# Keeping split weights in DRAM for the second half of the tokens

## The chip, the cores and the metric

One core of one Trainium2 chip runs the kernel. The metric is the time of one execution on the device, in microseconds; of several runs the median is given. The engines are TensorE (PE in the profile, its weight loads PEld), VectorE (DVE), ScalarE (ACT), GpSimd (POOL) and SyncE (SP). SP computes nothing here: it issues most of the DMAs, in its own order, and waits before each until what that DMA needs is there.

## The reference

It is one layer of a decoder trunk over 2048 tokens of width 1024. A normalized input is multiplied by one wide matrix, and the columns go to four recurrent mixers, whose outputs are gated, merged by a second matrix and normalized.

```python
u = rmsnorm(h, norm_w[l])
proj = (u @ w_in[l]).astype(f32)
...
y_a = gla_branch(a_q, a_k, a_v, a_gr, a_z, ...)
y_b = mlstm_branch(b_q, b_k, b_v, b_i, b_f, b_o, b_z, ...)
y_c = hgrn2_branch(c_q, c_f, c_i, c_z, lower_bounds[l], ...)
y_d = ssd_branch(d_x, d_B, d_C, d_dt, d_z, ...)
mixed = jnp.concatenate([y_a, y_b, y_c, y_d], axis=-1)
h = h + mixed @ w_out[l]
return rmsnorm(h, final_norm_w)
```

Everything is float32. The mixers run in chunks, with a state carried from one to the next.

## The kernel before, in words

**Products in three passes.** TensorE takes operands of a rounded float32 type (F32R). To keep the accuracy, each matrix is split: hi is the rounded value, lo the rounded rest (value minus hi). A product is then the sum of three matmuls, hi with hi, hi with lo and lo with hi, accumulated in PSUM. The input is split into `uh` and `ul`, the weights into `hi` and `lo`.

**Two halves.** The loop over `self.hf` in `run` takes the tokens in two halves of 1024. Each half runs ten units in the order g0, g1 (GLA), s0, s1 (SSD), h0 to h3 (HGRN2), m0, m1 (mLSTM). The projection columns stand in groups of 256, `("gqk", 0)`, `("gv", 0)` and so on, 30 for each half. Group `("gv", 0)` has 32 more columns for the gates (`wg`), so 288. The weights of a group are [128, 8, 256] float32, 1 MB, 8 KB in each partition. Both halves need the same weights. After the halves, the output stage multiplies by the second matrix.

**Loading a group.** `weights(key)` gives the split weights of a group and at once calls `load_w` for the next group of `worder`. `load_w` loads `raw` by a DMA on SP (line 224, for the gates 226), casts it to `hi` by four instructions on ACT (line 228) and subtracts to `lo` by two on POOL (line 230). There is one `raw` buffer and there are two each of `hi` and `lo`, so the split of a group waits for TensorE to have left the buffers of the group before last. The very first group comes in five pieces (lines 216 to 220), between the loads of the input tiles `xT` (line 153), which land in the small shared buffers `t2k`, of which there are five.

**The mixers.** In `lin_unit` (GLA, HGRN2) DVE multiplies `kb` and `qf` by decays (lines 496, 497), TensorE makes score tiles, and DVE and ACT put them into `ST`. In `ssd` DVE makes the decay tile at line 884, ACT the exponential at 885, DVE the product at 886, and TensorE goes on with that; each pass needs the next `ab` load (line 859). In `mlstm` line 766 copies the state. `store` (line 616) sends finished tiles from a `t2k` buffer to `y` in DRAM. `gates` holds a scan on DVE (line 363). The statistics of the rows (`row_stats`, line 169) need eight x tiles before the first projected values can be scaled.

**What sets the order.** The code's order is not the engines' order. The framework places each engine's instructions by its own estimate of when they can run, so the projection of the next group is mixed with the recurrence of the unit before it. Each engine, and SP with its DMAs, then runs its list strictly in order.

Of the kernel before, what the change touches and what calls it, by code (L numbers as in the profile page):

```python
# [10 lines left out]
F32 = mybir.dt.float32  # L11
F32R = mybir.dt.float32r
# [9 lines left out]
P = 128  # L22
S = 2048
D = 1024
KT = D // P
# [7 lines left out]
WG = 256  # L33
NG = 32
# [11 lines left out]
def _groups():  # L46
    g = {}
    cols = []

    def add(key, c):  # L50
        g[key] = len(cols)
        cols.append(c)

    for p in range(2):
        add(("gv", p), _r(GV + 256 * p, 256))
        add(("gqk", p), _r(GQ + 128 * p, 128) + _r(GK + 128 * p, 128))
        add(("gz", p), _r(GZ + 256 * p, 256))
    for h in range(4):
        add(("hqf", h), _r(HQ + 128 * h, 128) + _r(HF + 128 * h, 128))
        add(("hvz", h), _r(HV + 128 * h, 128) + _r(HZ + 128 * h, 128))  # L60
    for h in range(4):
        add(("mqk", h), _r(MQ + 128 * h, 128) + _r(MK + 128 * h, 128))
        add(("mvo", h), _r(MV + 128 * h, 128) + _r(MO + 128 * h, 128))
        if h % 2 == 0:
            add(("mz", h // 2), _r(MZ + 128 * h, 256))
    for q in range(2):
        add(("sx", q), _r(SX + 256 * q, 256))
        add(("sbc", q), _r(SB + 128 * q, 128) + _r(SC + 128 * q, 128))
        add(("sz", q), _r(SZ + 256 * q, 256))
    return g, cols  # L70


GIDX, GCOLS = _groups()
# [43 lines left out]
class Kernel:  # L117
# [79 lines left out]
    def weights(self, key):  # L197
# [4 lines left out]
            self.load_w(self.worder[nxt][1])  # L202
        return w

    def load_w(self, key, cuts=None):

        nc = self.nc
        gates = key == ("gv", 0)
        n = WG + (NG if gates else 0)
        raw = self.wp.tile([P, KT * (WG + NG)], F32, tag="raw", name="raw")[:, :KT * n].rearrange("p (k n) -> p k n", k=KT)  # L210
        hi = self.wp.tile([P, KT * (WG + NG)], F32R, tag="hi", name="hi", bufs=2)[:, :KT * n].rearrange("p (k n) -> p k n", k=KT)
        lo = self.wp.tile([P, KT * (WG + NG)], F32R, tag="lo", name="lo", bufs=2)[:, :KT * n].rearrange("p (k n) -> p k n", k=KT)
        self.wready[key] = hi, lo

        def part(k0, k1):
            nc.sync.dma_start(raw[:, k0:k1, :WG], self.a["w"][GIDX[key], :, k0:k1])
            if gates:
                nc.sync.dma_start(raw[:, k0:k1, WG:], self.a["wg"][:, k0:k1])
            nc.scalar.copy(hi[:, k0:k1], raw[:, k0:k1])
            nc.gpsimd.tensor_tensor(lo[:, k0:k1], raw[:, k0:k1], hi[:, k0:k1].bitcast(F32), op=ALU.subtract)  # L220

        if cuts:
            return [(k0, lambda k0=k0, k1=k1: part(k0, k1)) for k0, k1 in zip(cuts, cuts[1:] + [KT])]
        nc.sync.dma_start(raw[:, :, :WG], self.a["w"][GIDX[key]])
        if gates:
            nc.sync.dma_start(raw[:, :, WG:], self.a["wg"])
        for k0, k1 in ((0, 2), (2, 4), (4, 6), (6, 8)):
            nc.scalar.copy(hi[:, k0:k1], raw[:, k0:k1])  # L228
        for k0, k1 in ((0, 4), (4, 8)):
            nc.gpsimd.tensor_tensor(lo[:, k0:k1], raw[:, k0:k1], hi[:, k0:k1].bitcast(F32), op=ALU.subtract)  # L230

    def proj_chan(self, w, c, b):

        hi, lo = w
        ps = self.psp.tile([P, 512], F32, tag="proj", name="ps_c")
        cs = slice(c * P, (c + 1) * P)
        for k in range(KT):
            self.mm(ps, hi[:, k, cs], self.uh[b][:, k], start=k == 0, stop=False)
            self.mm(ps, hi[:, k, cs], self.ul[b][:, k], start=False, stop=False)
            self.mm(ps, lo[:, k, cs], self.uh[b][:, k], start=False, stop=k == KT - 1)  # L240
        return ps
# [770 lines left out]
    def run(self, units=None, y=None):  # L1012
        nc, tc, a = self.nc, self.tc, self.a
        pool = tc.tile_pool
        with pool(name="const", bufs=1) as cp, pool(name="small", bufs=2) as self.small, pool(name="dram", bufs=1, space=DRAM) as self.dram:
            self.y = self.dram.tile([S // P, 4, 32, DI // P, 4, 32], F32, tag="y", name="y") if y is None else y
            cf = cp.tile([P, 3 * P], F32, name="cf")
            self.ident, self.tri, self.cmask = (cf[:, i * P:(i + 1) * P] for i in range(3))
            self.mask = cp.tile([P, 768], U8, name="mask")
            self.par = cp.tile([P, a["par"].shape[1]], F32, name="par")  # L1020
            nc.sync.dma_start(self.par, a["par"])
            with pool(name="main", bufs=1) as self.up, pool(name="gs", bufs=1) as self.gs, pool(name="ps", bufs=1, space=PSUM) as psp:
                self.psp = _Tags(psp, {"proj": 4, "t": 4})
                self.up = _Tags(self.up, {"f": 2, "kb": 2, "qp": 2, "v": 2, "sz": 4})
                with pool(name="u", bufs=2) as self.upool, pool(name="w", bufs=1) as self.wp:
                    self.zero(cp)
                    self.whole = units is None
                    us = units or ["g0", "g1", "s0", "s1", "h0", "h1", "h2", "h3", "m0", "m1"]
                    keys = []
                    for u in us:  # L1030
                        j = int(u[1])
                        keys += {"g": [("gqk", j), ("gv", j), ("gz", j)], "h": [("hqf", j), ("hvz", j)], "s": [("sx", j), ("sbc", j), ("sz", j)],
                                 "m": [("mqk", 2 * j), ("mvo", 2 * j), ("mqk", 2 * j + 1), ("mvo", 2 * j + 1), ("mz", j)]}[u[0]]
                    self.worder = [(hf, k) for hf in range(NH) for k in keys]
                    self.wready = {}
                    self.stats = {}
                    self.xs = {}
                    first = self.load_w(keys[0], [0, 1, 2, 4, 6])
                    for self.hf in range(NH):
                        for b in range(2):  # L1040
                            if (self.hf, b) not in self.xs:
                                self.load_x(self.hf, b, first if (self.hf, b) == (0, 0) else ())
                        self.uh, self.ul = ([self.xs[self.hf, b][i] for b in range(2)] for i in range(2))
                        if self.hf == 0:
                            nc.sync.dma_start(cf, a["cf"][:, :3 * P])
                            self.prepare(cp)
                        for u in us:
                            self.steps = self.row_stats(self.hf + 1, ["f"] * NC, 1) if u == us[-1] and self.hf + 1 < NH else iter(())
                            {"g": self.gla, "h": self.hgrn, "m": self.mlstm_pair, "s": self.ssd}[u[0]](int(u[1]))
                            for _ in self.steps:  # L1050
                                pass
                if units is None:
                    with pool(name="wo", bufs=1) as wo:
                        self.out_phase(wo)
# [89 lines left out]
```

## Time and profile before

| | us |
|---|---|
| median of 3 runs | 2236.55 (2234.35 to 2238.48) |
| the profiled execution | 2236.62 |
| its span, first to last instruction | 2234.8 |
| first half of the tokens | 0 to 949 |
| second half | 949 to 1876 |
| output stage | 1876 to 2234.8 |

The profiled execution stands for the runs: it lies 0.07 us from their median. Its span is 1.8 us shorter than its time. A row of the timeline gives the start and the duration in us, the engine, the line, the operation, what it writes and from what, and in square brackets how long the engine stood idle before it and who released it. "x3" means that neighbouring rows of one kind are merged. SPq is SP's issuing of a DMA; its duration includes the waits between merged issues. The granted clock of TensorE is a share of its full 2.4 GHz; its lower level is 1.2 GHz.

### The profile page before, as it was taken

How to read it: one execution, taken by the hardware profiler on the slowest of the kernel's cores; microseconds unless marked ns; L12 is line 12 of the kernel's file. 1: busy time of each engine (PE TensorE's matmuls, PEld its weight loads, DVE VectorE, ACT ScalarE, POOL GpSimd, SP SyncE). 2: the span in 40 equal slices, each digit the busy share in tenths (PEclk: the TensorE clock that was granted, in tenths of full speed). 3: DMA queues.
4: the chain of work that ended last, by engine and by line, in shares of the span. 5: the costliest groups of instructions: out<-in, count | busy, mean ns of one | idle time of the engine just before them, and what ended most of it. 6: DMA issues, size and time to landing. Idle time of an engine off the chain costs nothing.

```text
span 2234.8 us, 35049 instructions
## 1 busy us (share of the span) xinstructions
PE 2113.7 (95%) x13758; PEld 1888.7 (85%) x13758; DVE 1395.2 (62%) x3325; ACT 821.5 (37%) x1763; POOL 382.7 (17%) x283
## 2 busy tenths in 40 slices
PE   8899999989999999998989899999999999999998
PEld 7888788878889998997978788888899998788887
DVE  3674878767667676636677876776676566532332
ACT  6633332344434334454323223443343334321211
POOL 3212122320111111121211222211111210000000
PEclk9999999999999999999999989999999999999999
DMA  7111212221111132420202222211121215432321
GB/s 235 56 34 44 58 47 66 69 48 48 49 49 39 49 84 106 126 75 22 58 24 62 69 46 76 54 36 43 45 76 49 56 48 175 160 111 78 113 71 48
DMA packets 186149, 156.66 MB, mean 70 GB/s; under 512 B 141944, under 2 KB 154344, under 8 KB 178688
## 3 DMA queue, kind: packets, MB, share of 16 engines
q1 hardware_dynamic: 179504, 135.02, 21.2%
q10 hardware_dynamic: 6480, 19.40, 2.4%
q8 instruction: 108, 1.77, 0.3%
q14 instruction: 57, 0.47, 0.1%
HBM read 129.11 MB, written 25.27 MB: 69 GB/s over the span
## 4 chain that ended last, share of the span: by engine, by line
PE 75%; DVE 16%; ACT 4%; DMA 2%; issue 2%; POOL 0%; SPq 0%; ACTq 0%; DVEq 0%
PE ps_t L123 26%; PE ps_c L123 19%; PE ps_out L123 15%; PE ps_o L123 6%; PE ps_s L123 4%; PE ps_u L123 2%; PE ps_g L123 2%; DVE t2k L884 2%; DVE kb L496 2%; DVE qf L497 1%; DVE xc L717 1%; DMA ST<-w_out 1%; DMA t2k<-xT 1%; DVE st L766 1%; DMA ab<-rows 1%
## 5 line engine op out<-in xcount | busy, mean ns | idle before, releaser
L123 PE MATMUL ps_t<-hi,uh 128*128 128x256 f32 x1920 | 546.5, 285 | 0.0
L123 PE MATMUL ps_t<-hi,ul 128*128 128x256 f32 x1920 | 546.0, 284 | 0.0
L123 PE MATMUL ps_t<-lo,uh 128*128 128x256 f32 x1920 | 545.1, 284 | 0.0
L230 POOL TENSOR_TENSOR lo<-raw,hi 128x1024 fp32r<-128x1024 f32 (+1 forms) x118 | 294.4, 2515 | 950.2 <-ACT hi L228 917.3
L123 PEld LDWEIGHTS ps_t<-lo,uh 128*128 128x128 f32 x1920 | 369.8, 193 | 0.9
L123 PEld LDWEIGHTS ps_t<-hi,uh 128*128 128x128 f32 x1920 | 369.6, 193 | 1.0
L123 PEld LDWEIGHTS ps_t<-hi,ul 128*128 128x128 f32 x1920 | 369.5, 192 | 1.0 <-issue 0.9
L123 PE MATMUL ps_c<-uh,hi 128*128 128x512 f32 x896 | 357.9, 400 | 7.4 <-ACT uh L155 7.4
L123 PE MATMUL ps_c<-uh,lo 128*128 128x512 f32 x896 | 358.6, 400 | 0.0
L123 PE MATMUL ps_c<-ul,hi 128*128 128x512 f32 x896 | 357.7, 399 | 0.0
L123 PEld LDWEIGHTS ps_c<-uh,hi 128*128 128x128 f32 x896 | 171.5, 191 | 40.4 <-ACT uh L155 7.8
L123 PEld LDWEIGHTS ps_c<-ul,hi 128*128 128x128 f32 x896 | 171.6, 191 | 34.7 <-DVE ul L156 0.5
L123 PEld LDWEIGHTS ps_c<-uh,lo 128*128 128x128 f32 x896 | 171.1, 191 | 33.5
L228 ACT CAST hi<-raw 128x512 fp32r<-128x512 f32 (+1 forms) x236 | 134.6, 626 | 59.6 <-issue 33.2
L956 DVE TENSOR_TENSOR o_sz<-o_sz,ps_out 128x512 f32<-128x512 f32 (+1 forms) x33 | 22.1, 671 | 130.5 <-PE ps_out L123 127.9
L123 PE MATMUL ps_out<-woh,o_qp 128*128 128x512 f32 x288 | 94.0, 394 | 0.0
L281 ACT ACTIVATE v<-ps_t,ss 128x128 f32<-128x128 f32 x128 | 39.7, 361 | 129.3 <-PE ps_t L123 129.0
L276 ACT ACTIVATE sz<-ps_t,ss 128x128 f32<-128x128 f32 (+1 forms) x160 | 53.2, 387 | 65.2 <-PE ps_t L123 58.1
L123 PE MATMUL ps_out<-woh,o_v 128*128 128x512 f32 (+1 forms) x213 | 75.4, 389 | 0.0
L277 DVE SCALAR_TENSOR_TENSOR sz<-sz,ps_t 128x256 f32<-128x256 f32 (+1 forms) x80 | 37.5, 469 | 60.7 <-ACT sz L276 60.4
L497 DVE TENSOR_TENSOR qf<-qf,pl 128x512 f32<-128x512 f32 x72 | 61.0, 847 | 21.6 <-ACT t2k L472 12.1
L496 DVE TENSOR_TENSOR kb<-kb,pl 128x512 f32<-128x512 f32 x72 | 67.9, 942 | 10.3 <-PE ps_s L123 9.4
(367 smaller groups left out, 3793.1 us busy)
## 6 DMA issues: line engine op xcount, KB each, us to landing
raw<-w SPq DMA_DIRECT2D x59, 1024.0 KB, 4.8
y<-t2k SPq DMA_DIRECT2D x256, 64.0 KB, 2.0
t2k<-y SPq DMA_DIRECT2D x64, 256.0 KB, 3.5
t2k<-xT SPq DMA_DIRECT2D x32, 256.0 KB, 3.6
ab<-rows SPq DMA_DIRECT2D x16, 512.0 KB, 5.0
o_sz<-x ACTq DMA_DIRECT2D x16, 512.0 KB, 4.5
o_f<-x SPq DMA_DIRECT2D x12, 512.0 KB, 5.3
mb<-rows SPq DMA_DIRECT2D x8, 512.0 KB, 3.6
```

What stands on the lines that cost most here:

```text
L123: self.nc.tensor.matmul(out, l, r, start=start, stop=stop, skip_group_check=shared)
L228: nc.scalar.copy(hi[:, k0:k1], raw[:, k0:k1])
L230: nc.gpsimd.tensor_tensor(lo[:, k0:k1], raw[:, k0:k1], hi[:, k0:k1].bitcast(F32), op=ALU.subtract)
L276: nc.scalar.activation(out[:, j], ps[:, j], AF.Tanh, scale=self.rsh[:, t + j:t + j + 1])
L277: nc.vector.scalar_tensor_tensor(out=out, in0=out, scalar=1.0, in1=ps, op0=ALU.add, op1=ALU.mult)
L281: self.nc.scalar.activation(out[:, j], ps[:, j], AF.Identity, scale=sc[:, t + j:t + j + 1])
L496: nc.vector.tensor_tensor(kv[:, :, 0], kv[:, :, 0], pv[:, :, 1:2].to_broadcast([P, n, b]), op=ALU.mult)
L497: nc.vector.tensor_tensor(qv[:, :, 1], qv[:, :, 1], pv[:, :, 0:1].to_broadcast([P, n, b]), op=ALU.mult)
L717: nc.vector.scalar_tensor_tensor(out=acc, in0=raw[:, k:k + TH], scalar=cw[k], in1=acc, op0=ALU.mult, op1=ALU.add)
L766: nc.vector.tensor_copy(st[:, 0, :N], car)
L884: nc.vector.scalar_tensor_tensor(out=L[:, h], in0=ab[:, h, j * C:(j + 1) * C], scalar=self.acs[:, cc, 4 * q + h:4 * q + h + 1], in1=self.c ...
L956: nc.vector.tensor_tensor(xt[:, ns], xt[:, ns], ps, op=ALU.add)
```

## The change

In the first half each group is split as before, and then `hi` and `lo` are written to scratch tensors in DRAM (`wk`, one pair per group), by two DMAs on SP. In the second half the same group finds its pair in `self.wkept`, and two DMAs on SP load `hi` and `lo` directly; there is no raw load, no cast on ACT and no subtraction on POOL. The pieces of the very first group are stored piece by piece.

```diff
+    def ahead_of(self, key):
+
+        return int(key in self.wkept)
...
         n = WG + (NG if gates else 0)
-        raw = self.wp.tile([P, KT * (WG + NG)], F32, tag="raw", name="raw")[:, :KT * n].rearrange("p (k n) -> p k n", k=KT)
...
         self.wready[key] = hi, lo
+        if self.ahead_of(key) > 0:
+            for t, d in zip((hi, lo), self.wkept[key]):
+                nc.sync.dma_start(t.bitcast(F32), d.bitcast(F32))
+            return
+        raw = self.wp.tile([P, KT * (WG + NG)], F32, tag="raw", name="raw")[:, :KT * n].rearrange("p (k n) -> p k n", k=KT)
+        self.wkept[key] = [self.dram.tile([P, KT, n], F32R, tag=f"wk{GIDX[key]}{i}", name="wk") for i in range(2)]
...
             nc.gpsimd.tensor_tensor(lo[:, k0:k1], raw[:, k0:k1], hi[:, k0:k1].bitcast(F32), op=ALU.subtract)
+            keep(k0, k1, 0)
+            keep(k0, k1, 1)
+
+        def keep(k0, k1, i):
+            nc.sync.dma_start(self.wkept[key][i][:, k0:k1].bitcast(F32), (hi, lo)[i][:, k0:k1].bitcast(F32))
...
             nc.scalar.copy(hi[:, k0:k1], raw[:, k0:k1])
+        keep(0, 8, 0)
         for k0, k1 in ((0, 4), (4, 8)):
             nc.gpsimd.tensor_tensor(lo[:, k0:k1], raw[:, k0:k1], hi[:, k0:k1].bitcast(F32), op=ALU.subtract)
+        keep(0, 8, 1)
...
+                    self.wkept = {}
```

The instructions move on each engine accordingly. In the changed kernel a line number is some 16 higher (line 616 becomes 632, 230 becomes 245, 695 becomes 711). At the start of the program SP's list before held, from the third piece of the first group on, raw pieces and input tiles alone:

```order
L216 DMA raw<-w 128x512
L153 DMA t2k<-xT 128x512 x2
L216 DMA raw<-w 128x512
L153 DMA t2k<-xT 128x512 x2
L216 DMA raw<-w 128x512
L153 DMA t2k<-xT 128x512 x5
```

The same place of SP's list now, from the fourth piece on (three stores of hi stand just ahead of these rows):

```order
L225 DMA raw<-w 128x512
L153 DMA t2k<-xT 128x512 x2
L225 DMA raw<-w 128x512
L234 DMA wk<-hi 128x512
L234 DMA wk<-lo 128x256 x2
L234 DMA wk<-lo 128x512 x2
L234 DMA wk<-hi 128x512
L234 DMA wk<-lo 128x512
L153 DMA t2k<-xT 128x512 x5
```

The seventh input tile, the first of the last row, now follows the stores of all pieces. Further on, of the eight x tiles of the row statistics three stand ahead of the stores of the gate group and five behind them.

At the change from the first half to the second, SP's list before loaded the raw weights of the gate group first, then input tiles (xT) and finished outputs (y):

```order
L224 DMA raw<-w 128x8x256
L226 DMA raw<-wg 128x8x32
L153 DMA t2k<-xT 128x512 x8
L616 DMA y<-t2k 32x16x32 x8
L153 DMA t2k<-xT 128x512 x5
L224 DMA raw<-w 128x2048
L153 DMA t2k<-xT 128x512 x3
L616 DMA y<-t2k 32x16x32 x8
```

There SP now has (2304 elements is the gate group, 2048 another group):

```order
L219 DMA hi<-wk 128x2048
L153 DMA t2k<-xT 128x512 x8
L632 DMA y<-t2k 32x16x32 x8
L153 DMA t2k<-xT 128x512 x5
L219 DMA hi<-wk 128x2304
L153 DMA t2k<-xT 128x512 x3
L632 DMA y<-t2k 32x16x32 x8
L219 DMA lo<-wk 128x2304
```

Lo of the gate group has moved behind the last eight stores, and TensorE's list has two products of that group 18 products ahead of the end of the group before it. In the second half, POOL's list before held subtractions among its other work (here from GLA to SSD):

```order
L471 MEMSET t2k 64x4x64 x6
L230 TENSOR_TENSOR lo<-raw,hi 128x1024 x2
L471 MEMSET t2k 64x4x64 x2
L230 TENSOR_TENSOR lo<-raw,hi 128x1024 x2
L695 MEMSET ST_93 128x4x128
L695 MEMSET ST_95 128x4x128
L230 TENSOR_TENSOR lo<-raw,hi 128x1024 x4
L896 TENSOR_TENSOR t2k<-t2k 128x256
L897 TENSOR_TENSOR sz<-t2k,sz 128x256
```

The same stretch of POOL's list now:

```order
L487 MEMSET t2k 64x4x64 x26
L711 MEMSET ST_93 128x4x128
L711 MEMSET ST_95 128x4x128
L912 TENSOR_TENSOR t2k<-t2k 128x256
L913 TENSOR_TENSOR sz<-t2k,sz 128x256
```

All subtractions are gone from there; the other work of POOL stands in the same order.

## Rows read from the trace of the kernel before

**Rows 1.** Busy time by stage: stretch, length, engines' busy us, granted clock, DMA share, GB/s.
```profile
0.00:949.00 949.00, 888.64 (x6133) 807.20 (x6134) 637.69 (x1505) 385.28 (x834) 204.75 (x155) 0.98 0.24 71
949.00:1876.00 927.00, 874.35 (x6069) 796.06 (x6068) 625.29 (x1461) 356.41 (x779) 177.94 (x128) 0.98 0.20 55
```
**Rows 2.** Whom TensorE waited for, 949 to 1876: us in total, times, longest us.
```profile
PE ps_o L123 <- DVE t2k L886: 13.3, 7, 3.8
PE ps_s L123 <- DVE kb L496: 7.5, 3, 3.4
PE ps_s L123 <- ACT t2k L439: 5.7, 4, 1.9
PE ps_m L386 <- DVE o_sz L363: 5.6, 1, 5.6
PE ps_u L123 <- ACT t2k L569: 4.4, 2, 4.0
...
PE ps_u L123 <- DVE rs_y L135: 4.2, 3, 1.5
```
**Rows 3.** POOL's costliest group, 949 to 1876: busy us, mean ns, idle before, releasers.
```profile
L230 POOL TENSOR_TENSOR lo<-raw,hi 128x1024 fp32r<-128x1024 f32 x56 | 139.2, 2506 | 464.5 <-ACT hi L228 461.4 <-issue 1.5 <-DVE qf L497 1.2
```
**Rows 4.** Timeline in SSD of the second half, a split beside line 884.
```profile
1226.56 4.75 POOL L230 TENSOR_TENSOR lo<-raw,hi 128x1024 fp32r<-128x1024 f32 x2 [19.26 <-ACT hi L228]
...
1226.96 4.76 DVE L884 SCALAR_TENSOR_TENSOR t2k<-ab,g_cs,cf 128x128 f32<-128x128 f32 x3
...
1233.16 1.47 PE L123 MATMUL ps_o<-t2k 128*128 128x64 f32 x8 [3.77 <-DVE t2k L886]
...
1238.98 0.60 DVE L884 SCALAR_TENSOR_TENSOR t2k<-ab,g_cs,cf 128x128 f32<-128x128 f32 x2
```
**Rows 5.** Timeline in mLSTM of the second half, POOL and DVE.
```profile
1654.19 4.74 POOL L230 TENSOR_TENSOR lo<-raw,hi 128x1024 fp32r<-128x1024 f32 x2 [19.46 <-ACT hi L228]
...
1657.11 1.91 DVE L766 COPY st<-mst 128x129 f32<-128x129 f32 x1 [0.40 <-PE ps_o L123]
...
1666.11 0.23 DVE L766 COPY st<-mst 128x129 f32<-128x129 f32 x1
```
**Rows 6.** Timeline in HGRN2 of the second half, DVE; POOL splits from 1466.57 on.
```profile
1467.60 1.91 DVE L496 TENSOR_TENSOR kb<-kb,pl 128x512 f32<-128x512 f32 x1
...
1474.04 0.70 DVE L496 TENSOR_TENSOR kb<-kb,pl 128x512 f32<-128x512 f32 x1
```
**Rows 7.** The page, DMA issues: count, KB of one, median us to landing.
```profile
raw<-w SPq DMA_DIRECT2D x59, 1024.0 KB, 4.8
...
t2k<-xT SPq DMA_DIRECT2D x32, 256.0 KB, 3.6
...
out_dram<-o_sz SPq DMA_DIRECT2D x16, 256.0 KB, 3.3
```
**Rows 8.** The chain of work that ended last: start us, us, what.
```profile
32.53 2.64 POOL lo L230
35.21 27.31 PE ps_g L123 x191
...
962.83 25.21 PE ps_g L123 x189
...
1683.34 23.03 PE ps_t L123 x192
```
**Rows 9.** Timeline of the start: SP, POOL and DVE.
```profile
8.84 6.48 SPq L153 DMA_DIRECT2D t2k<-xT  x5
...
14.41 1.70 POOL L220 TENSOR_TENSOR lo<-raw,hi 128x512 fp32r<-128x512 f32 x1 [0.66 <-ACT hi L219]
...
36.57 0.42 SPq L169 DMA_DIRECT2D o_pl<-x  x1
...
45.07 0.17 DVE L176 TENSOR_SCALAR ss<-ss 128x8 f32<-128x8 f32 x1 [14.09 <-ACT o_pl L173]
```
**Rows 10.** Timeline of the stage change: SP's last eight y stores.
```profile
955.29 5.28 SPq L616 DMA_DIRECT2D y<-t2k  x8
```

## The prediction

> **What bounds the kernel now.** The first view to read is the busy time by stage [rows 1]: TensorE is busy for 874.35 of the 927 us of the second half of the tokens and for 888.64 of 949 in the first; the output stage behind them the change doesn't touch. So the kernel is bound by TensorE, and an edit can win only what TensorE stands idle, 52.65 us in the second half, and what its clock costs. The granted clock there is 0.98 on average; between 2.4 GHz and 1.2 GHz this means some 4% of 927 us, 37 us, at the lower level, and about 18 us lost by it.
>
> The second view is who TensorE waits for in the second half [rows 2]: VectorE (DVE) and ScalarE (ACT), never GpSimd (POOL). One could conclude that the work which the change removes, 139.2 us of POOL in this stretch [rows 3] and the casts on ACT, costs nothing. The timelines say otherwise. At 1226.56 POOL begins the two subtractions of a split, and in the same 4.75 us DVE gets only three score instructions of line 884 done, 4.76 us in all; the same instruction takes 0.60 us for two when POOL is quiet, at 1238.98. TensorE, which needs that score tile, then idles 3.77 us [rows 4]. In the mLSTM part the copy of line 766 takes 1.91 us beside a split and 0.23 without [rows 5]; in HGRN2 the product of line 496 takes 1.91 us while a split runs and 0.70 a moment later [rows 6]. POOL is thus on the path through DVE, and each split is charged to TensorE in places.
>
> The Trainium skill has this as a rule ("SBUF — State Buffer", section "Who interferes with whom"): a VectorE instruction with two SBUF inputs, or in a two-port mode, and a GpSimd instruction that reads SBUF take a shared port pair as an exclusive lock, so the later one stands still. The trace agrees: 4.76 us for three against 0.60 for two. The same section says that DMA never contends with an engine; by it the loads that replace the splits would hold nobody, and the holds of the second half would all go.
>
> **The change part by part.**
>
> *Splits of the second half.* All 30 groups lose four casts on ACT and two subtractions on POOL. What TensorE gets back I take wait by wait [rows 2], by whether a split lies just before it: of the 13.3 us behind line 886 three of seven waits, the longest shown in rows 4, 9 us; of 7.5 and 5.7 behind lines 496 and 439 most, 11; of the 5.6 behind line 363, where the scan and a copy before it are both held, 4; of the 4.4 behind line 569, where DVE is behind by two held instructions, 4; of the 4.2 behind line 135, which follow the held copy of line 766, 4. That is 32 us. Of the 18 us of clock I take a third, 6, since the low stretches follow TensorE's long idle spells and only some of these go. From 38 I take off 3, since behind a released wait the next input is sometimes late too: **35 us gained**. Bounds: 18, if half of the waits are taken over by the next input, and 58, all of the 52.65 us and a third of the clock.
>
> *Loads instead.* Each group now waits for TensorE to leave the buffers of the group before last and then loads twice 1 MB. A 1 MB load takes 4.8 us to land [rows 7], two 9.6. Between release and first use lies a whole group, at least the 23.03 us of 192 products [rows 8]. Price nothing; without that cover it would be what exceeds it, up to 9.6 us for a group.
>
> *Stores at the start.* Here the queue's order decides. SP used to send the seventh x tile at 8.84 us; now the five pieces of the first group's hi and lo are stored ahead of it, and the last waits for POOL's fifth subtraction, which ended at 14.41 + 1.70 = 16.1 us. The tile goes out 8 us later. TensorE gets to it only after six others, so I charge 4 us (2 to 8). The same again for the row statistics: five of the eight x tiles stand behind the store of the gate group's lo, whose second half is subtracted until 32.53 + 2 times 2.64 = 37.8 us, 4 more by the delay above. The last tile then leaves near 44.5 instead of 36.57 us, behind 2.4 MB of stores, and the sum of squares that was used at 45.07 comes 8 to 12 us later. TensorE has four PSUM tiles of cover, half of the 27.31 us from 35.21 on, until 48.9, which the delay moves to 53. A stall of 5 (2 to 9). With 1 us for the small gate loads behind the next store: **10 us lost**, 4 to 18 [rows 8, 9].
>
> *The stage change.* Lo of the second half's gate group stands on SP behind eight y stores, issued from 955.29 for 5.28 us, so it lands near 960.6 + 4.8 = 965.4. TensorE now has two products of that group 18 products (4 us) before the point where it began it in earnest, 962.83 [rows 8, 10], so it wants lo at 958.7. Of the 6.7 us between them some 2.5 go as the stores come earlier, DVE being held no more. **4 us lost**, 0 to 8.
>
> *Stores later in the first half.* SP was already blocked until POOL was done, since the next raw load waits for it; the stores stand in the same place, so their waits cost nothing new. What is new is 2 MB in the queue ahead of the next raw load, 9.6 us by the landing time of a load. No row has a 1 MB store; the nearest is 256 KB from SBUF to the output, 3.3 us to land against 3.6 for a load of an x tile of that size [rows 7], so I price a store as a load. The raw load has a group's time of cover [rows 8]. A y store or an ab load behind the burst lands later and holds its buffer longer: **3 us lost**, 0 (all within slack) to 12 (four places at 3 us).
>
> The Trainium skill speaks against this part ("DMA: Bandwidth & Descriptors", section "Anatomy of one DMA — SWDGE (gpsimd) path"): a semaphore wait happens on the issuing sequencer before dispatch, and a completion can be surprisingly late when the target is HBM. The first half agrees with SP's waits at the start [rows 9]; by the second, which no run here shows at this size, the burst would be dearer, as in the first rival.
>
> **The sum**, against the profiled execution's own 2236.62 us (span 2234.8 and 1.8 around it; the median of the runs is 2236.55, the same): 2236.62 - 35 + 10 + 4 + 3 = 2218.6, or **2219 us**.
>
> **The rivals.**
> 1. *Slower: the bursts hold the one queue.* Place: the first half, where y stores and ab loads follow a store pair and a raw load within some microseconds. For it: there is one queue, and few t2k buffers, each held until its store has landed. Against it: the DMA share there is only 0.24 [rows 1]. Priced at eight places of 3 us, with the upper ends 18 and 8: 2236.6 - 35 + 18 + 8 + 24 = 2252. It decides once a y store stays out longer than DVE takes to need its buffer again.
> 2. *No difference: the next input is as late.* DVE, ACT and TensorE feed each other in turn in these stages, so a freed DVE may wait for ACT. Then the gain is its lower bound: 2236.6 - 18 + 17 = 2236.
> 3. *More: all idle time of the second half goes*, since a backlog of DVE also reaches waits without a split beside them: 2236.6 - 58 + 12 = 2191, with the start at 7 and 5 for the rest.
> 4. *It doesn't do what it says: loads come late*, because SP stands at another wait when the buffers come free. At 2 us for each of 30 groups: 2236.6 - 35 + 17 + 60 = 2279. Against it: 9.6 us in 23.03.
>
> **How the numbers follow.** Forecast 0.62 (its own range 2207 to 2231, all faster), rival 1 0.12, rival 2 0.13, rival 3 0.10, rival 4 0.03. A measurement of this kernel can tell about 0.2%, 4.5 us, from no change. Faster: 0.62 + 0.10 = 0.72; within: 0.13; slower: 0.12 + 0.03 = 0.15. The range goes from 2199, which leaves out most of rival 3, to 2248, which leaves out over half of rival 1 and rival 4, together under 0.2.
>
> **What would show it.** In the profile after, POOL is busy under 45 us in the second half and lines 884, 766 and 496 keep their short times there; TensorE's idle time in that half falls from 53 to about 25 us, while in the first 75 us it rises by some 10. Wrong it is if TensorE's waits of the second half keep their sum with other names (rival 2), if TensorE waits for DMA on hi or lo at more places than the stage change (rival 4), or if the first half after 100 us is longer by more than 12 us (rival 1).

## The result, and the profile after

The changed kernel takes 2197.4 us (median of four runs, 2196.05 to 2200.29) against 2236.6 us before (2234.35 to 2238.48): a ratio of 0.9826, with a 95% interval of 0.9813 to 0.9839, or 39 us. It was forecast faster, but by 17.6 us; the time lies just below the range of 2199 to 2248. The profiled execution after is the slowest of the four (2200.29 us); its span is 2198.2 us, 36.6 less than that of before, and the steps below add up to this 36.6.

Both lists of TensorE hold the same products, so the two traces can be cut where it begins the same group of weights: the gz group of the first half, the first group of the second half, its fourth group, and its last. The busy times of before in these four stretches, as in [rows 1]:

```profile
0.00:62.40 62.40, 52.53 (x290) 46.99 (x290) 20.51 (x52) 34.50 (x59) 19.97 (x23) 0.97 0.64 215
62.40:938.70 876.30, 825.80 (x5801) 751.70 (x5800) 611.10 (x1447) 347.36 (x767) 179.42 (x130) 0.98 0.21 59
938.70:1013.50 74.80, 73.41 (x498) 68.33 (x496) 32.72 (x55) 40.45 (x68) 18.11 (x14) 1.00 0.29 89
1013.50:1839.70 826.20, 775.05 (x5342) 701.51 (x5342) 567.36 (x1314) 302.32 (x678) 165.19 (x116) 0.98 0.19 52
```

The same four stretches after (columns as in [rows 1]: length, busy TensorE, its weight loads, DVE, ACT, POOL, each with its instructions, then granted clock, DMA share, GB/s):

```profile
0.00:78.50 78.50, 58.38 (x290) 50.07 (x291) 19.34 (x52) 34.36 (x60) 19.55 (x23) 0.91 0.76 262
78.50:953.30 874.80, 828.96 (x5800) 753.96 (x5799) 608.06 (x1447) 345.93 (x762) 173.03 (x128) 0.98 0.37 123
953.30:1034.50 81.20, 76.71 (x496) 70.62 (x496) 23.20 (x49) 32.91 (x53) 3.31 (x8) 0.96 0.38 124
1034.50:1804.00 769.50, 758.47 (x5344) 687.49 (x5343) 492.43 (x1322) 250.73 (x577) 35.18 (x64) 1.00 0.30 92
```

TensorE's instruction counts agree within two, so the lengths can be subtracted: the start is 16.1 us longer, the rest of the first half 1.5 shorter, the stage change 6.4 longer, the second half from there 56.7 shorter, and what follows 0.9 shorter. Each difference also splits into the time that TensorE stands idle (length less busy) and the time that it is busy with the same products, in which a lower granted clock shows:

| stretch | difference, us | idle | busy |
|---|---|---|---|
| start | +16.1 | 9.87 to 20.12, +10.25 | +5.85, clock 0.97 to 0.91 |
| rest of first half | -1.5 | 50.50 to 45.84, -4.7 | +3.2 |
| stage change | +6.4 | 1.39 to 4.49, +3.1 | +3.3, clock 1.00 to 0.96 |
| second half | -56.7 | 51.15 to 11.03, -40.1 | -16.6, clock 0.98 to 1.00 |

In the second half the instructions that stood beside a split are short again. Minimum, median and maximum of a line's duration in ns, after; before, the maxima of these three lines were 2500, 1917 and 2854, at about the same medians [rows 4 to 6]:

```profile
L900 DVE SCALAR_TENSOR_TENSOR t2k<-ab,g_cs,cf x64: 332/343/656, 1226.8 to 1380.8; 128x128 f32<-128x128 f32 x64
L782 DVE COPY st<-mst x7: 228/230/232, 1593.6 to 1762.7; 128x129 f32<-128x129 f32 x7
L512 DVE TENSOR_TENSOR kb<-kb,pl x36: 681/686/734, 1055.1 to 1574.0; 128x512 f32<-128x512 f32 x36
```

And of TensorE's waits there [rows 2] these are the longest, 1034.5 to 1804 (total us, times, longest); the 13.3 us of seven waits for line 886, now line 902, have shrunk to 1.3:

```profile
PE ps_s L123 <- DVE kb L512: 5.3, 4, 2.2
PE ps_o L123 <- DVE t2k L902: 1.3, 4, 0.4
PE ps_m L402 <- DVE o_sz L379: 1.3, 1, 1.3
```

The start pays for it. In the timeline of SP after, the five input tiles from the seventh on go out at 19.76, not at 8.84 [rows 9]. They stand behind the stores of the first group's pieces, and the row statistics' last x tiles, which go out from 46.40 on, stand behind the store of the gate group's lo:

```profile
16.08 1.87 SPq L234 DMA_DIRECT2D wk<-lo  x4
...
19.76 2.34 SPq L153 DMA_DIRECT2D t2k<-xT  x5
...
46.02 0.33 SPq L234 DMA_DIRECT2D wk<-lo  x1
46.40 0.43 SPq L169 DMA_DIRECT2D o_kb<-x  x1
```

The stores of the first group's pieces (L234, for casts of line 228 and subtractions of line 229) held SP for ACT's casts far more than for POOL (who waited for whom, in the first 80 us: us in total, times, longest):

```profile
SPq L234 <- ACT hi L228: 8.0, 4, 4.5
SPq L234 <- POOL lo L229: 0.8, 1, 0.8
```

Each store of hi waits for its cast, and the fourth raw piece, behind three of them, goes out at 9.09 and not at 4.49. Its cast then begins at 15.01 and not at 11.72, and what follows it comes later too.

TensorE's waits of the first 80 us after are below. Those for uh (the input) were 6.0 us before. The one of ps_rb, which transposes the row statistics, is new; the profile puts it down to a cast on ACT, but DVE had finished the row statistics only then, too.

```profile
PE ps_c L123 <- ACT uh L155: 10.2, 3, 6.0
PE ps_rb L188 <- ACT hi L242: 4.2, 1, 4.2
PE ps_g L123 <- POOL lo L245: 3.6, 2, 2.9
```

At the stage change lo of the gate group leaves SP behind the eight y stores, at 975.98, and TensorE waits 2.5 us for it:

```profile
969.96 5.97 SPq L632 DMA_DIRECT2D y<-t2k  x8
975.98 0.50 SPq L219 DMA_DIRECT2D lo<-wk  x1
```
```profile
PE ps_g L123 <- DMA lo<-wk: 2.5, 1, 2.5
```

What the forecast had undervalued above all is the clock. Its loss before was not spread over the second half. It lies in the first 331.5 us of the stretch, in GLA and SSD; behind that the clock is 1.00, though TensorE idles there too, 18.5 us in all (2.7 us is the longest spell):

```profile
1013.50:1345.00 331.50, 298.85 (x2067) 265.02 (x2067) 236.42 (x518) 103.57 (x211) 72.17 (x66) 0.94 0.19 48
1345.00:1413.00 68.00, 64.06 (x410) 57.31 (x409) 45.26 (x120) 28.93 (x64) 20.98 (x18) 1.00 0.27 75
1413.00:1613.00 200.00, 189.68 (x1312) 171.49 (x1311) 139.43 (x338) 84.15 (x198) 30.62 (x13) 1.00 0.17 44
1613.00:1840.00 227.00, 222.77 (x1560) 207.99 (x1559) 146.54 (x340) 85.78 (x207) 41.42 (x19) 1.00 0.19 57
```

From 1229 on, for instance, TensorE is busy for 0.40 of 4 us (it waits at the place of [rows 4]). In the stretches behind that the granted clock is 0.62 and 0.86, so part of them ran at 1.2 GHz and not at 2.4:

```profile
1229.00:1233.00 4.00, 0.40 (x2) 0.00 (x0) 3.31 (x4) 0.63 (x1) 2.31 (x1) 1.00 0.22 37
1233.00:1236.00 3.00, 2.84 (x12) 2.57 (x13) 0.48 (x3) 0.00 (x0) 0.00 (x0) 0.62 0.75 306
1236.00:1240.00 4.00, 4.00 (x20) 3.32 (x19) 3.60 (x12) 0.65 (x2) 1.57 (x2) 0.86 0.00 0
```

The same happens at the start of the kernel after, behind the new wait of ps_rb:

```profile
60.00:64.00 4.00, 1.41 (x6) 1.22 (x7) 2.08 (x14) 3.74 (x9) 2.47 (x2) 0.77 0.22 92
64.00:68.00 4.00, 4.00 (x18) 4.00 (x18) 0.00 (x0) 0.02 (x1) 2.21 (x1) 0.50 0.69 274
```

The page's DMA issues after show what a 1 MB store takes to land, which no row of before had [rows 7]; a 1 MB load now takes 6.7 to 6.9 us where it took 4.8:

```profile
raw<-w SPq DMA_DIRECT2D x29, 1024.0 KB, 6.9
lo<-wk SPq DMA_DIRECT2D x29, 1024.0 KB, 6.8
hi<-wk SPq DMA_DIRECT2D x29, 1024.0 KB, 6.7
wk<-hi SPq DMA_DIRECT2D x28, 1024.0 KB, 3.9
wk<-lo SPq DMA_DIRECT2D x28, 1024.0 KB, 4.8
```

### The profile page after: what moved, and what is told of

Its sections match the earlier page's. It is cut to its first block, busy times and chain, and to the rows that moved or that the text cites. A ratio compares the mean times of both kernels' runs of the same rounds, so it can differ in the third digit from the quotient of the medians.

```text
span 2198.2 us, 35026 instructions
## 1 busy us (share of the span) xinstructions
PE 2108.9 (96%) x13758; PEld 1883.2 (86%) x13758; DVE 1306.8 (59%) x3325; ACT 761.0 (35%) x1643; POOL 231.1 (11%) x223
## 4 chain that ended last, share of the span: by engine, by line
PE 79%; DVE 12%; ACT 4%; DMA 2%; issue 1%; SPq 0%; POOL 0%; ACTq 0%; DVEq 0%; POOLq 0%
PE ps_t L123 27%; PE ps_c L123 20%; PE ps_out L123 16%; PE ps_o L123 6%; PE ps_s L123 5%; PE ps_u L123 2%; PE ps_g L123 2%; DVE t2k L900 1%; DVE kb L512 1%; DMA t2k<-xT 1%; DVE xc L733 1%; DVE qf L513 1%; DVE t2k L611 1%; DMA raw<-w 0%; DVE ST L557 0%
## 5 line engine op out<-in xcount | busy, mean ns | idle before, releaser
L245 POOL TENSOR_TENSOR lo<-raw,hi 128x1024 fp32r<-128x1024 f32 (+1 forms) x58 | 143.2, 2489 | 451.3 <-ACT hi L242 451.2
L293 DVE SCALAR_TENSOR_TENSOR sz<-sz,ps_t 128x256 f32<-128x256 f32 (+1 forms) x80 | 37.7, 471 | 75.3 <-ACT sz L292 74.8
L242 ACT CAST hi<-raw 128x512 fp32r<-128x512 f32 (+1 forms) x116 | 65.9, 626 | 37.4 <-PE ps_c L123 20.9
L123 PEld LDWEIGHTS ps_out<-woh,o_qp 128*128 128x128 f32 x288 | 54.2, 188 | 12.8
L513 DVE TENSOR_TENSOR qf<-qf,pl 128x512 f32<-128x512 f32 x72 | 54.7, 759 | 17.7 <-PE ps_s L123 9.8
```

Of the source, the lines that this page charges most:

```text
L123: self.nc.tensor.matmul(out, l, r, start=start, stop=stop, skip_group_check=shared)
L293: nc.vector.scalar_tensor_tensor(out=out, in0=out, scalar=1.0, in1=ps, op0=ALU.add, op1=ALU.mult)
L513: nc.vector.tensor_tensor(qv[:, :, 1], qv[:, :, 1], pv[:, :, 0:1].to_broadcast([P, n, b]), op=ALU.mult)
```

## The experiments

All times are medians of four runs, beside runs of the kernel before on the same chip (medians 2235.3 to 2236.6; the experiments ran on three chips). Line numbers differ a little from kernel to kernel. Lengths of stretches are cut at the same groups of weights as above. "The second half" is the stretch of 826.2 us before and 769.5 after.

### Which engine's absence pays: lo alone kept, hi alone kept

Theory A: POOL's subtractions hold DVE, and DVE holds TensorE. Rival B: the casts on ACT, which the change also removes, are what held. The first kernel takes away POOL's part alone, the second ACT's alone. In both the first half is the changed kernel's.

```diff
-            for t, d in zip((hi, lo), self.wkept[key]):
-                nc.sync.dma_start(t.bitcast(F32), d.bitcast(F32))
...
+            nc.sync.dma_start(raw[:, :, :WG], self.a["w"][GIDX[key]])
...
+            nc.sync.dma_start(lo.bitcast(F32), self.wkept[key][1].bitcast(F32))
+            for k0, k1 in ((0, 2), (2, 4), (4, 6), (6, 8)):
+                nc.scalar.copy(hi[:, k0:k1], raw[:, k0:k1])
```

> The first half is that of the changed kernel. In the second half only lo is loaded from scratch; the raw weights are loaded and cast to hi on ACT as before the change. So only POOL's subtractions are gone there, and ACT keeps its 116 casts (about 66 us). Theory A (POOL's subtractions hold DVE, which holds TensorE): the whole gain of the second half stays, 2197 to 2206 us. Rival B (ACT's casts are what held the outputs up, since a score or an output that ACT copies waits behind them): most of the 58 us gained in the second half is gone, 2235 to 2255 us.

```diff
-            for t, d in zip((hi, lo), self.wkept[key]):
-                nc.sync.dma_start(t.bitcast(F32), d.bitcast(F32))
+            nc.sync.dma_start(hi.bitcast(F32), self.wkept[key][0].bitcast(F32))
...
+            nc.sync.dma_start(raw[:, :, :WG], self.a["w"][GIDX[key]])
...
+            for k0, k1 in ((0, 4), (4, 8)):
+                nc.gpsimd.tensor_tensor(lo[:, k0:k1], raw[:, k0:k1], hi[:, k0:k1].bitcast(F32), op=ALU.subtract)
```

> The first half is that of the changed kernel. In the second half only hi is loaded from scratch; the raw weights are loaded too, and POOL subtracts lo as before the change. ACT's casts alone are gone. Theory A (POOL's subtractions hold DVE): nearly all of the 58 us gained in the second half is lost again, 2240 to 2255 us. Rival B (ACT's casts are what held): the gain stays, 2197 to 2210 us.

Measured: 2191.4 us (2188.5 to 2193.8) with lo alone, 2281.3 us (2279.1 to 2281.6) with hi alone. The second half of the first kernel, then of the second:

```profile
1028.20:1797.00 768.80, 758.25 (x5345) 687.16 (x5343) 492.48 (x1322) 303.91 (x681) 35.20 (x64) 1.00 0.31 91
```
```profile
1042.00:1885.40 843.40, 786.10 (x5345) 711.95 (x5343) 573.54 (x1316) 249.81 (x576) 169.06 (x116) 0.96 0.28 83
```

With lo alone the second half has the length of the changed kernel's, though ACT is busy 304 us there and not 251: the casts cost TensorE nothing there. The time lies below what theory A had given, 2197 to 2206 us, because the stage change is 74.6 us long and not 81.2. With hi alone it is longer than before the change, 843.4 against 826.2, though ACT has less to do. Rival B falls in both, and theory A holds in its direction.

But 2281.3 us is more than the 2240 to 2255 that A gave: the same subtractions cost 75 us here (843.4 less 768.8) and 57 before (826.2 less 768.8), and the stage change is 9.4 us longer than before. What differs is when they run. Before, POOL waited for ACT's casts; here it waits mostly for the load of hi:

```profile
L224 POOL TENSOR_TENSOR lo<-raw,hi 128x1024 fp32r<-128x1024 f32 (+1 forms) x58 | 149.5, 2598 | 499.9 <-DMA hi<-wk 378.2 <-PE ps_o L123 53.8 <-PE ps_c L123 38.3
```

So they meet other DVE instructions. In mLSTM TensorE's waits for line 135 (the reciprocal square root, a chain of small DVE instructions) were 4.2 us for three before and are 12.0 us for three here. That this other place explains the whole extra time was not tested by itself.

### Does POOL hold DVE when it only writes?

The kernel with hi alone kept, with fills in place of the subtractions:

```diff
             for k0, k1 in ((0, 4), (4, 8)):
-                nc.gpsimd.tensor_tensor(lo[:, k0:k1], raw[:, k0:k1], hi[:, k0:k1].bitcast(F32), op=ALU.subtract)
+                for r in ((k0, k1), (k0, k1), (k0, k0 + 2)):
+                    nc.gpsimd.memset(lo[:, r[0]:r[1]].bitcast(F32), 0.0)
```

> As the run that keeps hi alone, but POOL fills lo of the second half with zeros at the same place, five fills of about 0.5 us (128x512) in place of each 2.4 us subtraction, so it leaves lo of the second half's weights out of the result and is busy about as long. Theory A in its narrow form (POOL holds DVE only while it reads SBUF): 2197 to 2208 us. Rival C (any work of POOL in SBUF at that place holds DVE, or a lo that comes later than a load would bring it holds TensorE): 2235 to 2255 us, as with the subtraction.

Measured: 2197.2 us (2194.3 to 2200.7). (It has six fills a group, not the five announced: four of about 0.95 us and two of 0.53.) The second half is 773.3 us long with POOL busy 154 us in it, nearly as long as before the change (165). Copies are still held beside a fill: the copy of line 737 (715 before) takes up to 3.6 us and not 0.17. The product of line 518 (496 before), with two inputs, is not, though five of its 36 stood beside fills (minimum, median, maximum in ns):

```profile
L737 DVE COPY halo<-craw x16: 160/170/3629, 1153.2 to 1778.7; 128x3 f32<-128x3 f32 x16
```
```profile
L518 DVE TENSOR_TENSOR kb<-kb,pl x36: 678/684/731, 1049.9 to 1572.9; 128x512 f32<-128x512 f32 x36
```

The longest of these copies was let go at 1287.29, when the last of six fills in a row ended (1282.68 and 4.58 us); others ended with an earlier fill. The score instructions that stand behind it in DVE's order end with it too.

```profile
1282.68 4.58 POOL L225 MEMSET lo<- 128x1024 f32 x6 [4.68 <-PE ps_c L123]
1283.66 3.63 DVE L737 COPY halo<-craw 128x3 f32<-128x3 f32 x1
```

Against the kernel with lo alone kept, 4.5 us of the second half remain of 57. So it is not that POOL is busy, and what fits is that it reads. The fills also run at other times, since they wait for TensorE and not for a cast, and each is shorter than a subtraction, so this run alone does not separate reading from place or length. The Trainium skill ("SBUF — State Buffer", section "Who interferes with whom") says that a DVE instruction with two SBUF inputs contends with a GpSimd instruction that reads SBUF and not with one that only writes it, while a copy, where it runs in a two-port mode, contends with GpSimd in any case. The rows of lines 518 and 737 agree, 731 ns at most for the one and 3629 for the other.

### The stores by themselves

```diff
-        return int(key in self.wkept)
+        return 0
...
+        store = key not in self.wkept
...
+            if store:
+                nc.sync.dma_start(self.wkept[key][i][:, k0:k1].bitcast(F32), (hi, lo)[i][:, k0:k1].bitcast(F32))
```

> The first half stores hi and lo as the changed kernel does, and the second half splits the raw weights again as before the change. It prices the stores by themselves. By the traces of before and after, the first products of the gz group came 16 us later and stayed 15 to 16 us later through the first half: if that is the stores' own price, and the second half's gain is that of the missing splits, 2236.6 + 16 = 2253 us (2248 to 2258). If the late start came from elsewhere (another order of the scheduler's around the loads), about 2237 us.

Measured: 2251.6 us (2248.9 to 2251.8), ratio 1.0066 (1.0049 to 1.0083): 15.2 us slower than before, as the first alternative had it. The gz group begins at 76.8, 14.4 us later than before, and at the last group of the second half the delay is 16.3. The rest of the first half pays 1.8 us for 2 MB of stores a group, and the second half is that of before to the tenth of a microsecond:

```profile
1029.80:1856.00 826.20, 775.02 (x5343) 701.52 (x5342) 567.63 (x1314) 302.52 (x678) 165.24 (x116) 0.98 0.19 52
```

### The price of the start: order or bytes

Each group's stores are issued when its products begin, behind the loads of the next group, and no longer straight after the split. The second kernel does the same with lo alone, as in the kernel that keeps lo alone.

```diff
             self.load_w(self.worder[nxt][1])
+        self.store_w(key, w)
         return w
+    def store_w(self, key, w):
+        if self.hf == 0:
+            for i in (0, 1):
+                self.nc.sync.dma_start(self.wkept[key][i].bitcast(F32), w[i].bitcast(F32))
...
-        keep(0, 8, 0)
...
-        keep(0, 8, 1)
```

> The changed kernel, but each group's hi and lo are stored when TensorE's products of that group begin, not straight after the split; on SP's list the input tiles of the first pass now stand ahead of the first stores. If the 16 us lost at the start come from the order (input tiles that wait on SP behind stores which wait for ACT and POOL): about 2184 us (2180 to 2189), and 53 us less than before the change. If they come from the bytes of the stores beside the loads: 2193 to 2199, no change against the changed kernel.

> Only lo is kept, as in the run that keeps lo alone (2191.4 us), stored when the products of its group begin; hi is cast again in the second half. By the order theory of the start 13 to 16 us less than that run: 2175 to 2180 us. By the theory of bytes half of the stores and so half of the 16: 2183.

Measured: 2190.7 us (2184.5 to 2191.9) and 2181.8 us (2181.0 to 2184.2), that is 6.7 us less than the changed kernel and 9.6 less than the kernel with lo alone kept. The gz group begins at 67.9 and at 63.6, 5.5 and 1.2 us later than before the change. In the first, which stores as much as the changed kernel, the seventh input tile goes out at 9.31 again and TensorE's waits for uh are back to 5.8 us. The second stores half as much, and its start runs at the full clock:

```profile
0.00:63.60 63.60, 51.76 (x290) 45.53 (x290) 20.39 (x52) 34.57 (x59) 19.86 (x23) 1.00 0.79 263
```

So in the profiles 10.6 of the 16.1 us were the order of SP's list, with the same bytes. The rest can't be told from chance here: the kernel below that splits on DVE in the second half alone has the start of the kernel before, instruction for instruction, and its profile shows the gz group at 67.1 and not at 62.4:

```profile
0.00:67.10 67.10, 54.64 (x289) 48.22 (x290) 24.43 (x52) 34.56 (x59) 19.88 (x23) 0.92 0.61 200
```

The first kernel's median fell by 6.7 us only. It lies between its two expectations, above the 2180 to 2189 of the order theory; the rest of its first half is 2.1 us longer than in the changed kernel (876.9 against 874.8).

### The stage change

```diff
-                nc.sync.dma_start(t.bitcast(F32), d.bitcast(F32))
+                (nc.scalar if gates else nc.sync).dma_start(t.bitcast(F32), d.bitcast(F32))
```

> The changed kernel, with the gate group's hi and lo of the second half issued from ACT's queue and not from SP's, so that they don't stand behind the last eight y stores. If the 6.7 us lost at the stage change are lo standing behind those stores: 2197.4 - 6.5 = 2191 us. If lo is late because its buffer comes free late or the transfer itself is long, or if ACT is held up as much: 2196 to 2200.

Measured: 2191.4 us (2189.9 to 2194.4), 6 us less than the changed kernel, as expected. The stage change is back to about its length of before (74.8), and TensorE's wait for lo is gone:

```profile
950.10:1024.60 74.50, 73.11 (x496) 68.20 (x495) 23.33 (x50) 32.96 (x53) 3.31 (x8) 1.00 0.41 135
```

### What DVE pays for the same subtractions

If POOL's subtractions hold DVE, DVE might as well do them. First in the first half, with lo kept and stored late; then with smaller pieces on POOL instead.

```diff
         for k0, k1 in ((0, 4), (4, 8)):
-            nc.gpsimd.tensor_tensor(lo[:, k0:k1], raw[:, k0:k1], hi[:, k0:k1].bitcast(F32), op=ALU.subtract)
+            nc.vector.tensor_tensor(lo[:, k0:k1], raw[:, k0:k1], hi[:, k0:k1].bitcast(F32), op=ALU.subtract)
```

> As the run that keeps lo alone and stores it late, but in the first half DVE does the subtractions (two per group of 1024 elements, about 1.1 us each by DVE's 0.6 us for 512, 65 us in all) in place of POOL. If the loss lies in that POOL holds DVE at any moment for 2.4 us (80 us of held time in the first half), DVE's own shorter work costs TensorE less: 2160 to 2172 us. If what counts is the time that DVE is not free, it is about the same: 2172 to 2182.

```diff
-        for k0, k1 in ((0, 4), (4, 8)):
+        for k0 in range(KT):
+            k1 = k0 + 1
             nc.gpsimd.tensor_tensor(lo[:, k0:k1], raw[:, k0:k1], hi[:, k0:k1].bitcast(F32), op=ALU.subtract)
```

> As the run that keeps lo alone and stores it late, but in the first half POOL subtracts in eight pieces of 256 elements (about 0.6 us) in place of two of 1024 (2.4 us). If a held DVE instruction waits for one POOL instruction only and then goes ahead, the longest hold falls to 0.6 us and most of the first half's 80 us of held time goes: 2150 to 2170 us. If DVE stays held until POOL has nothing more to do, or POOL takes the port again at once: as without it, 2174 to 2182.

Measured: 2131.5 us (2128.4 to 2133.9) with DVE, 2160.4 us (2158.8 to 2164.6) with small pieces, against 2181.8 without either. DVE's gain of 50 us is beyond both expectations. Its group of subtractions in the first half, and the first half without its start:

```profile
L251 DVE TENSOR_TENSOR lo<-raw,hi 128x1024 fp32r<-128x1024 f32 x54 | 65.5, 1221 | 3.1 <-ACT hi L249 2.9
```
```profile
65.60:891.00 825.40, 812.00 (x5801) 741.22 (x5800) 586.25 (x1500) 349.13 (x767) 38.72 (x73) 1.00 0.35 98
```

One takes 1.22 us, half of POOL's 2.41. DVE is busy 586 us in this stretch against 611 before: hardly less, while TensorE's idle time falls from 50.5 to 13.4 us and its clock rises to 1.00. So the share of time in which DVE is busy is not what costs. Small pieces bring less than half of that, 21 us, which the first alternative allowed for (2150 to 2170):

```profile
67.10:925.80 858.70, 826.64 (x5801) 752.14 (x5800) 583.64 (x1446) 347.27 (x767) 222.83 (x290) 0.98 0.34 94
```

A piece on POOL takes 0.74 us, so most holds are shorter, but the eight pieces take 5.9 us a group and not 4.8. What DVE loses beside splits in the first half falls from 84 to 58 us only (an estimate from the two traces: each instruction's excess over the median of its form), so most of the held time did not go. These pieces, shorter than the fills above but reading, leave the stretch 33 us longer than DVE's subtractions do (858.7 against 825.4), where the fills, in the other half, cost 4.5. So the length of POOL's instruction alone doesn't explain what the fills saved.

Then with DVE in place of POOL in the kernel before, in both halves or in the second alone; nothing is kept in either.

> The kernel before, nothing kept and nothing stored, with one word changed: DVE and not POOL subtracts lo, in both halves (the first group's five pieces stay on POOL). If all that the changed kernel gains is that POOL no longer holds DVE, the second half gains as much here as the first did when its subtractions moved to DVE (50 us): 2236 - 50 - 50 to 58 = 2128 to 2136 us, and keeping the weights brings nothing beyond. If the loads are worth more than that because DVE, ACT and the raw load have nothing to do for them: 2145 to 2160 us.

> The kernel before, nothing kept, with DVE in place of POOL for the subtractions of the second half alone. It is what the change does to POOL in that half without its stores and loads. If the stores at the start (16 us) and the late lo at the stage change (6.7 us) are the whole price of keeping, and POOL's absence the whole gain (58 us): 2236 - 58 = 2178 us, up to 2188 if DVE's own 65 us of subtractions cost a little. If the gain needed the loads: 2200 to 2236.

Measured: 2132.9 us (2132.5 to 2136.6), ratio 0.9546 (0.953 to 0.9561), with both halves on DVE, and 2184.8 us (2178.5 to 2186.1) with the second alone, both as the first alternative had it. The second half of the latter:

```profile
1017.90:1788.90 771.00, 758.01 (x5343) 687.57 (x5342) 545.06 (x1366) 302.75 (x677) 35.09 (x64) 1.00 0.20 55
```

Its length is 771.0 us against 769.5 with everything loaded. DVE does 63 us of subtractions there (52 of 1.22 us), ACT all its casts, and this costs 1.5 us. (DVE's busy time is 53 us more than in the changed kernel, 545 against 492, because some 10 us of its other work fall ahead of the cut here.) So of the 56.7 us that the change gained in the second half, 55.2 are to be had by moving the subtractions off POOL, without a scratch, a store or a load. The kernel that keeps lo and splits on DVE (2131.5) and the one that keeps nothing (2132.9) can't be told apart.

> As the run with DVE's subtractions in the first half and lo kept (2131.5 us), with four pieces of 512 elements in place of two of 1024, so that other DVE work waits at most half as long behind one. If DVE's own pieces still hold TensorE up in places: 2122 to 2130 us. If nothing waits for them any more: 2130 to 2134.

Measured: 2131.8 us (2130.3 to 2134.1) with four pieces of 512 elements on DVE, no change against 2131.5: smaller pieces there bring TensorE nothing.

## Why the prediction was wrong in size and right in its mechanism

*What bounds the kernel, and why.* POOL stands on none of TensorE's waits in the second half and yet on its path, through DVE. This is shown by the pair of runs with lo or hi alone kept, and by moving the subtractions to DVE.

*Splits of the second half, -35.* This is the step that failed, a term that was mis-sized: it measured -56.7, just inside its bound of -58. It had two parts. The waits were put at 32, less 3 for inputs that would be late next, and idle time fell by 40.1 us. The deduction of 3 had no counterpart; TensorE's waits for ACT there fell too, to 0.5 us, and rival 2 did not come true. The sum of waits had also left some out, these two above all, which [rows 2] doesn't show (949 to 1876, before):

```profile
PE ps_s L123 <- DVE qf L497: 4.3, 4, 1.4
PE ps_o L123 <- DVE halo L715: 2.9, 1, 2.9
```

The four waits behind line 497 each fell beside a split or within 2 us of its end, and all of them went. The one behind line 715 had no split within 8 us ahead of it, and yet it shrank to 0.6; so did most of the four waits behind line 886 that had been given nothing. Lines 496 and 439, on the other hand, gave back 7.9 of their 13.2 us and not 11.

The clock was put at 6 of 18, and busy time fell by 16.6. The argument was that only some of the low stretches would go, and it worked from the mean clock of the whole half. Cut into slices of 4 us, the trace before has a clock below 0.9 at nine places, all ahead of 1345 and each behind an idle spell, of 1.5 to 5.6 us; after, at one, around 1145. Seven of these nine spells were in the sum of waits, and the clock behind each should have gone into the sum with it.

*Loads instead, 0.* This was right: TensorE waits for hi or lo nowhere in the second half but at the stage change, though a load took 6.8 us to land and not 4.8. Rival 4 falls.

*Stores at the start, +10.* The idle time is this number, +10.25, in part by luck. The working let SP wait for POOL's fifth subtraction and sent the seventh tile out 8 us later; SP waited mostly for ACT's casts, and the tile went out 10.9 us later. The last x tile left at 49.87 where 44.5 was forecast, and the sum of squares was used 13.8 us later (58.90) and not 8 to 12. That SP's order costs there was right: moving the stores behind the input tiles gave 10.6 us back in the profile. The measured 16.1 also has 5.85 us more of busy time at a lower clock (0.91), for which there was no term. How much of that the stores cause stays open: five other kernels with these stores at the start are busy 56.9 to 59.6 us in it, the kernel with the start of before 54.64 and not 52.53.

*Stage change, +4.* The mechanism is shown by the run with the loads on ACT's queue. Idle time rose by 3.1 us, and again there was the clock, +3.3.

*Stores later in the first half, +3.* This measured -1.5 in the changed kernel and +1.8 in the run with stores alone, so next to nothing: there the one queue carries bursts of 2 MB a group, and TensorE hardly feels it. A store of 1 MB took 3.9 to 4.8 us to land, no dearer than the load it was priced by. The rule of the Trainium skill on late completions in HBM ("DMA: Bandwidth & Descriptors", section "Anatomy of one DMA — SWDGE (gpsimd) path") would have spoken for the first rival's 24 us, and these stores don't show it; that section is on DMAs that go through GpSimd, and these were issued by SP. Rival 1 falls.

*The rivals.* Rival 3, all idle time gone, came closest, 2191 for 2197, with a wrong division, so partly by luck: not all idle time went (11 of 51 us are left), and nearly all of the clock's share came back and not a third. Its reason, that waits without a split beside them go too, came out in part. It had a chance of 0.10.

Two things were thus mis-sized: the waits of the second half, by 11 us, and the clock, which was priced too low for the second half and not at all for the start and the stage change. With the clock as measured the forecast would have been 9 us higher for the start and the stage change and 11 us lower for the second half. Of the 18.6 us between the span's 36.6 and the forecast gain of 18, the second half makes 21.7; the other errors partly cancel (start 6.1 and stage change 2.4 dearer than forecast, the rest of the first half 4.5 cheaper).

## What to carry to other kernels

A helper engine that nobody waits for can still set the pace, by holding the engine that TensorE waits for; look for one instruction form with a short median and a long maximum, and see what runs beside the long ones. Price an idle spell of TensorE with the lower clock that follows it, if one does, read slice by slice at that place and not from the mean, both where an edit removes one and where it makes one. Before work is kept or moved through memory to spare an engine, try it on the engine that it holds up: here the subtractions took half the time each on that engine, and in its own order they cost 1.5 us of the second half where the holds had cost 57.

## What the runs showed of the hardware

DVE can be busy for nearly as long with work of its own as when it is held, and TensorE feels it far less. In the second half DVE was busy 545 us with its own subtractions (771.0 us long), 567 with POOL's (826.2) and 492 with none (769.5). A reading of these rows is that DVE's order puts its own subtractions where TensorE doesn't wait; no run tested that by itself.

POOL's subtraction of 1024 elements takes 2.41 us and DVE's 1.22, so that what was handed to the helper took twice as long there.

A held copy on DVE can outlast several of POOL's instructions: it took 3.63 us and ended with the last of six fills, four of 0.95 us and two of 0.53, that POOL ran one behind the other.
